# A third slot for split weights, and the two halves of a split issued in separate calls

## The chip, the cores and the metric

The kernel runs on one core of a Trainium2 chip. The metric is the device time in microseconds (us) of one execution; the figure for a kernel is the median of its runs. The engines of the core are named as in the profile: PE (matrix multiply), PEld (its weight loads, beside PE), DVE (vector), ACT (scalar), POOL (GpSimd) and SP (sync), from whose queue all DMAs here are issued.

## The reference

The reference computes, in fp32, two blocks over a sequence of 512 tokens with 1024 features, of which the first has two layers. It is cut here to what the matrix products are.

```
def first_block(x, mem, ...):                  # x: 512 x 1024, mem: 256 x 1024
    mem_n = rmsnorm(mem, mem_norm_g)
    for i in range(2):
        h = rmsnorm(x, norm_g[i])
        if i == 0: proj = h @ fox_w_in;  main = fox_attention(q, k, v, f_logit, b_f)
        else:      proj = h @ ret_w_in;  main = retention(q, k, v)
        memo = mem_cross_attention(q_mem, mem_n, w_mem_kv[i])
        x = x + (concat(main, memo) * silu(z)) @ w_out[i]
    return rmsnorm(x, final_norm_g)

def second_block(x, ...):
    h = rms_norm(x, norm_mix_pre)
    q, k, v, glu_in, gates = split(h @ w_in)
    y_a = dilated_attention(q, k, v, rel_bias) @ w_attn_out    # three groups, merged by their maxima and sums
    y_c = silu(layer_norm(causal_depthwise_conv(c_val * sigmoid(c_gate)))) @ conv_pw_w
    x = x + rms_norm((g_a * y_a + g_c * y_c) @ w_out, norm_mix_post)
    h = rms_norm(x, norm_ffn_pre)
    ...                                                         # gated FFN of width 2816, a conv of width 3
```

## The kernel before

Each fp32 product is made from three matmuls of split values: a value is its rounded high part h and the rest l, and a product sums h times h, h times l and l times h (mm3, L213 to L215; L422 to L424 for products laid out the other way round). Activations are split when they are written. Weights are split as they come: a job is one tile of weights of 1 MB. pump loads it (L314, on SP's queue) into one of two slots of ring_w; ACT copies it with rounding into the h half of a slot of ring_hl (L324, "the cast"), and DVE, for a few pieces POOL, subtracts that from the raw tile into the l half (L326, "the subtraction"). A job is split in two pieces as a rule. A slot of ring_hl holds h and l of a job, 2 x 2048 numbers of 4 bytes in each partition, 16 KiB; there are N_HL of them. When its last piece is split, the raw slot is free and pump loads the next job.

run_jobs goes through the list of jobs. A job with weights has one or more units, each a group of matmuls that fills a bank of psum and an evacuation of it. Before each unit and after the last one, cut_ahead(i, 1) splits one piece of a job to come, where a slot of ring_hl is free; after each unit, run_bg issues steps of background chains (norms, rotations, softmaxes, convolutions). This order of the text is not the final one: a scheduler puts the instructions on the queues of the engines, each of which then runs in order. Its result is what the rows of order in the section on the change show.

Places to which the text comes, by their lines:

- the first memory softmax, at 60 to 74 us: the exponentials L762 on ACT after a load of their table, the reciprocal L771 on DVE, the scaling L774 on POOL, and the transposes L782 on PE; L205 and L206 are a cast and a subtraction that split an activation, L876 a function of ACT in the chain of the forget gates;
- the entry to retention, at 528 to 570 us: L818 adds the last output projection of the first layer to x, L601 and L606 square and sum for the norm's statistic (L220 on PE, L230 on DVE, L231 on POOL), L519 and L694 split the memory's tiles, and the norm is applied to each of 8 tiles of x in L269 (product), L270 (its cast) and L271 (its subtraction, every second one on POOL); L678 adds projections;
- the exchanges of the three attention groups, four times from 1040 to 1345 us. They need maxima and sums of one group in the layout of another. Each writes them in L1541 and L1542 (to xn and xp in memory) and reads them back in L1547 and L1548, all on SP's queue; DVE makes coefficients from them (L1554 to L1563), POOL scales the probabilities with these (L1570), and PE transposes them (L1585). L1418 is the convolution on DVE, L1676 and L1682 store and fetch values of V in another order.

Of the kernel before, what the change touches and what calls it, by code (L numbers as in the profile page):

```python
# [11 lines left out]
F32 = mybir.dt.float32  # L12
# [22 lines left out]

N_R = 50
N_F = 23
N_HL = 2


class Slots:
# [59 lines left out]
def tile_kernel(ctx: ExitStack, tc: tile.TileContext, a: dict, out: bass.AP, stop_at=None):  # L101
    nc = tc.nc
# [8 lines left out]
    ring_w = cpool.tile([P, 2, 2048], F32, name="ring_w")  # L111
    ring_hl = cpool.tile([P, N_HL, 2, 2048], F32R, name="ring_hl")
    psum = ppool.tile([P, 8, 512], F32, name="psum")
# [3 lines left out]
    WS = Slots([ring_w[:, i] for i in range(2)], "W")  # L117
    WHL = Slots([ring_hl[:, i] for i in range(N_HL)], "WHL")
    PA = Slots([psum[:, i] for i in range(8)], "PA")
# [164 lines left out]
    chains = []  # L284
    once = deque()
    bg2 = deque()
    state = {"next": 0, "cut": 0, "rate": 1}

    def rate(n):
        state["rate"] = n  # L290
# [15 lines left out]
    def pump():  # L306

        while WS.q and state["next"] < len(weighted):
            j = weighted[state["next"]]
            state["next"] += 1  # L310
            j.w = WS.get()
            v = j.w.ap.rearrange("p (k c) -> p k c", k=j.shape[0])
            for sl, src in j.loads:
                nc.sync.dma_start(v[sl], src)  # L314

    def cut(j):

        if j.done == 0:
            j.s = WHL.get()
            j.hv = j.s.ap[:, 0].rearrange("p (k c) -> p k c", k=j.shape[0])  # L320
            j.lv = j.s.ap[:, 1].rearrange("p (k c) -> p k c", k=j.shape[0])
        v = j.w.ap.rearrange("p (k c) -> p k c", k=j.shape[0])
        sl = j.cut[j.done]
        nc.scalar.copy(j.hv[sl], v[sl])  # L324
        lo = j.hv[:, :, j.beside : 2 * j.beside] if j.beside else j.lv[sl]
        (nc.gpsimd if j.done in j.spare else nc.vector).tensor_sub(lo, v[sl], j.hv[sl].bitcast(F32))  # L326
        j.done += 1
        if j.done == len(j.cut):
            j.w.free()
            state["cut"] += 1  # L330
            pump()

    def cut_ahead(i, n):

        while n and state["cut"] < len(weighted) and state["cut"] <= i + 2:
            j = weighted[state["cut"]]
            if j.done == 0 and not WHL.q:
                return
            cut(j)
            n -= 1  # L340

    def run_bg():
        live = [c for c in chains if c.q]
        n = max(state["rate"], 1 if sum(len(c.q) for c in live) < 8 else 2)
        for c in live[:n]:
            c.q.popleft()()
        chains[:] = [c for c in chains if c.q]
        for _ in range(2):
            if once:
                once.popleft()()  # L350
        if bg2:
            bg2.popleft()()
# [7 lines left out]
    def run_jobs():  # L360
        i = -1
        for j in all_jobs:
            if j.loads is None:
                for u in j.units:
                    u()
                continue
            i += 1
            while state["cut"] <= i:
                cut(weighted[state["cut"]])
            if j.keep:  # L370
                continue
            for u in j.units:
                cut_ahead(i, 1)
                u(j.hv, j.lv)
                run_bg()
            for k in j.also + [j]:
                k.s.free()
            cut_ahead(i, 1)

    all_jobs = []  # L380
    weighted = []
# [1836 lines left out]
    weighted.extend(j for j in all_jobs if j.loads is not None)  # L2218
    prologue()
    run_jobs()  # L2220


# [53 lines left out]
```

## Time and profile before

| | |
|---|---|
| median of 3 runs | 1916.74 us (1914.56 to 1917.31) |
| the profiled execution | 1914.26 us, of which its span in the profile is 1912.5 us |
| PE busy | 1855.5 us, 97% of the span |
| DVE, ACT, POOL busy | 1134.0, 825.5 and 368.2 us |
| mean granted clock of PE | 0.990 |

Busy time is time in which an engine runs an instruction; the rest of its span it waits. The clock is given as a share of the full rate, 2.4 GHz. All places are given in us from the start of the span.

### The profile page before, as it was taken

What the parts mean: (1) busy time and instruction counts of PE and PEld (TensorE: products, weight loads), DVE (VectorE), ACT (ScalarE), POOL (GpSimd) and SP (SyncE); (2) the same over time, 40 slices, a digit from 0 to 9 for tenths busy, and PEclk for the clock granted to TensorE, in tenths of its full rate; (3) what the DMA queues carried; (4) which work ended last, traced back from release to release, by engine and by line L of the source; (5) the groups of instructions that cost most, each with busy time, mean ns of one, the idle gap of its engine ahead of it and who ended that gap; (6) DMA issues with size and microseconds to landing.
All of it is one profiled execution on the core that took longest, in us unless ns stands there. A gap on an engine that the chain in (4) does not pass through costs nothing. (4 is left out here: it accounts for less than half of the span.)

```text
span 1912.5 us, 24641 instructions
## 1 busy us (share of the span) xinstructions
PE 1855.5 (97%) x9759; PEld 1587.8 (83%) x9759; DVE 1134.0 (59%) x1752; ACT 825.5 (43%) x1389; POOL 368.2 (19%) x360
## 2 busy tenths in 40 slices
PE   7999999999989999999999998999899999999998
PEld 7788888888888888888878986988788887888886
DVE  7643543434474575755579797777365386554555
ACT  5544433444345545454353342335263455333342
POOL 1101000110131134333460202010131242100101
PEclk9999999999999999999999998999999999999999
DMA  6332322232233223323224432263553223323221
GB/s 207 115 119 87 100 77 89 79 99 91 86 114 101 94 78 100 100 77 99 67 72 145 137 100 72 59 179 68 167 170 113 89 67 101 109 88 111 88 90 65
DMA packets 200374, 194.57 MB, mean 102 GB/s; under 512 B 22200, under 2 KB 171575, under 8 KB 200259
## 3 DMA queue, kind: packets, MB, share of 16 engines
q1 hardware_dynamic: 200258, 193.00, 32.3%
q8 instruction: 76, 1.25, 0.3%
q14 instruction: 40, 0.32, 0.1%
HBM read 182.40 MB, written 12.94 MB: 102 GB/s over the span
## 5 line engine op out<-in xcount | busy, mean ns | idle before, releaser
L213 PE MATMUL psum<-arena_r,ring_hl 128*128 128x512 f32 (+1 forms) x1936 | 746.9, 387 | 1.8 <-ACT arena_r L1904 1.3
L215 PE MATMUL psum<-arena_r,ring_hl 128*128 128x512 f32 (+1 forms) x1936 | 740.1, 383 | 5.1 <-DVE ring_hl L326 5.1
L214 PE MATMUL psum<-arena_r,ring_hl 128*128 128x512 f32 (+1 forms) x1936 | 740.4, 383 | 3.4 <-DVE arena_r L627 2.6
L326 DVE TENSOR_TENSOR ring_hl<-ring_w,ring_hl 128x1024 fp32r<-128x1024 f32 (+2 forms) x306 | 394.6, 1296 | 303.0 <-ACT ring_hl L324 297.8
L324 ACT CAST ring_hl<-ring_w 128x1024 fp32r<-128x1024 f32 (+2 forms) x307 | 316.0, 1037 | 485.5 <-PE psum L214 315.4
L215 PEld LDWEIGHTS psum<-arena_r,ring_hl 128*128 128x128 f32 x1936 | 365.8, 189 | 77.3 <-DVE ring_hl L326 6.3
L214 PEld LDWEIGHTS psum<-arena_r,ring_hl 128*128 128x128 f32 x1936 | 366.4, 189 | 73.1 <-DVE arena_r L627 3.3
L213 PEld LDWEIGHTS psum<-arena_r,ring_hl 128*128 128x128 f32 x1936 | 366.3, 189 | 71.3 <-issue 1.9
L422 PE MATMUL psum<-ring_hl,arena_r 128*128 128x256 f32 x640 | 183.6, 287 | 2.2 <-ACT ring_hl L324 2.2
L424 PE MATMUL psum<-ring_hl,arena_r 128*128 128x256 f32 x640 | 182.9, 286 | 1.3 <-DVE ring_hl L326 1.3
L423 PE MATMUL psum<-ring_hl,arena_r 128*128 128x256 f32 x640 | 182.7, 285 | 0.0
L1418 DVE SCALAR_TENSOR_TENSOR arena_f<-cpad,vec,arena_f 128x512 f32<-128x512 f32 x240 | 173.8, 755 | 1.7
L422 PEld LDWEIGHTS psum<-ring_hl,arena_r 128*128 128x128 f32 x640 | 124.5, 194 | 3.4 <-ACT ring_hl L324 2.6
L424 PEld LDWEIGHTS psum<-ring_hl,arena_r 128*128 128x128 f32 x640 | 124.3, 194 | 1.8 <-DVE ring_hl L326 1.8
L423 PEld LDWEIGHTS psum<-ring_hl,arena_r 128*128 128x128 f32 x640 | 124.5, 194 | 0.5
L206 DVE TENSOR_TENSOR arena_r<-psum,arena_r 128x512 fp32r<-128x512 f32 (+2 forms) x136 | 79.3, 607 | 71.3 <-ACT arena_r L205 71.1
L205 ACT CAST arena_r<-psum 128x512 fp32r<-128x512 f32 (+2 forms) x136 | 66.9, 526 | 85.7 <-PE psum L215 35.2
L205 ACT CAST arena_r<-arena_f 128x512 fp32r<-128x512 f32 (+1 forms) x78 | 46.2, 598 | 117.0 <-POOL arena_f L1950 67.3
L926 POOL TENSOR_SCALAR arena_f<-arena_f,small 128x512 f32<-128x512 f32 (+3 forms) x48 | 34.1, 728 | 307.7 <-DVE small L924 302.4
L206 DVE TENSOR_TENSOR arena_r<-arena_f,arena_r 128x512 fp32r<-128x512 f32 (+1 forms) x78 | 53.3, 688 | 60.1 <-ACT arena_r L205 59.4
L606 POOL TENSOR_TENSOR arena_f<-arena_f 128x512 f32<-128x512 f32 x40 | 63.7, 1603 | 109.6 <-ACT arena_f L601 107.3
L1950 POOL TENSOR_TENSOR arena_f<-arena_f 128x512 f32<-128x512 f32 x22 | 32.0, 1456 | 262.2 <-DVE arena_f L1926 252.2
(238 smaller groups left out, 2093.3 us busy)
## 6 DMA issues: line engine op xcount, KB each, us to landing
ring_w<-in_fox_w_in SPq DMA_DIRECT2D x28, 1024.0 KB
ring_w<-in_w_in SPq DMA_DIRECT2D x22, 1024.0 KB
ring_w<-in_w_up SPq DMA_DIRECT2D x22, 1024.0 KB
ring_w<-in_w_out SPq DMA_DIRECT2D x20, 1024.0 KB
ring_w<-in_ret_w_in SPq DMA_DIRECT2D x16, 1024.0 KB
ring_w<-in_w_in SPq DMA_DIRECT2D x24, 512.0 KB
ring_w<-in_w_down SPq DMA_DIRECT2D x10, 1024.0 KB
ring_w<-in_w_mem_kv SPq DMA_DIRECT2D x8, 1024.0 KB
```

The lines of the kernel that those rows point to most:

```text
L205: nc.scalar.copy(h, src)
L206: nc.vector.tensor_sub(l, src, h.bitcast(F32))
L213: nc.tensor.matmul(ps, wh, xh, start=start and k == 0, stop=False, **o)
L214: nc.tensor.matmul(ps, wh, xl, start=False, stop=False, **o)
L215: nc.tensor.matmul(ps, wl, xh, start=False, stop=stop and k == n - 1, **o)
L324: nc.scalar.copy(j.hv[sl], v[sl])
L326: (nc.gpsimd if j.done in j.spare else nc.vector).tensor_sub(lo, v[sl], j.hv[sl].bitcast(F32))
L422: nc.tensor.matmul(o, c.h[:, sl], h[:, k, :], start=k == 0, stop=False)
L423: nc.tensor.matmul(o, c.l[:, sl], h[:, k, :], start=False, stop=False)
L424: nc.tensor.matmul(o, c.h[:, sl], l[:, k, :], start=False, stop=k == n - 1)
L606: nc.gpsimd.tensor_add(acc, acc, t.ap)
L1418: nc.vector.scalar_tensor_tensor(t, src, wk, t, ALU.mult, ALU.add)
```

## The change

There are three slots in ring_hl in place of two. The 16 KiB per partition for the third are taken from the scratch for dynamic DMAs, which is given 1024 bytes. The function cut is divided: cast() issues the cast of a piece and notes the piece in a list, halves; lower() takes the oldest from there and issues its subtraction. cut_ahead issues first the subtraction of the piece cast at the call before, and then the next cast. A job is cast if it lies at most two ahead of the running one, is loaded or being loaded, and has a slot. Every engine gets the same instructions as before. In the changed program lines above 313 keep their numbers; the cast is L326 (L324 before), the subtraction L338 (L326 before), and all later lines of the kernel have 14 more.

```diff
-N_HL = 2
+N_HL = 3
...
+    halves = deque()
+    state = {"next": 0, "cast": 0, "cut": 0, "rate": 1}
...
-    def cut(j):
-
+    def cast():
+
+        j = weighted[state["cast"]]
         if j.done == 0:
             j.s = WHL.get()
...
         sl = j.cut[j.done]
         nc.scalar.copy(j.hv[sl], v[sl])
-        lo = j.hv[:, :, j.beside : 2 * j.beside] if j.beside else j.lv[sl]
-        (nc.gpsimd if j.done in j.spare else nc.vector).tensor_sub(lo, v[sl], j.hv[sl].bitcast(F32))
+        halves.append((j, j.done))
         j.done += 1
         if j.done == len(j.cut):
+            state["cast"] += 1
+
+    def lower():
+
+        j, n = halves.popleft()
+        v = j.w.ap.rearrange("p (k c) -> p k c", k=j.shape[0])
+        sl = j.cut[n]
+        lo = j.hv[:, :, j.beside : 2 * j.beside] if j.beside else j.lv[sl]
+        (nc.gpsimd if n in j.spare else nc.vector).tensor_sub(lo, v[sl], j.hv[sl].bitcast(F32))
+        if n == len(j.cut) - 1:
             j.w.free()
             state["cut"] += 1
             pump()
 
     def cut_ahead(i, n):
 
-        while n and state["cut"] < len(weighted) and state["cut"] <= i + 2:
-            j = weighted[state["cut"]]
-            if j.done == 0 and not WHL.q:
-                return
-            cut(j)
+        while n:
             n -= 1
+            if halves:
+                lower()
+            c = state["cast"]
+            if c < len(weighted) and c <= i + 2 and c < state["next"] and (weighted[c].done or WHL.q):
+                cast()
...
             while state["cut"] <= i:
-                cut(weighted[state["cut"]])
+                if not halves:
+                    cast()
+                lower()
...
-    nc = bacc.Bacc("TRN2", target_bir_lowering=False, num_devices=1)
+    nc = bacc.Bacc("TRN2", target_bir_lowering=False, num_devices=1, dynamic_dma_scratch_size=1024)
```

On DVE, at the entry to retention, this stood from the norm's statistic L230 on (L326 is the subtraction of a piece of weights):

```order
L230 TENSOR_SCALAR small<-psum 128x4
L326 TENSOR_TENSOR ring_hl<-ring_w,ring_hl 128x8x128
L694 SCALAR_TENSOR_TENSOR arena_r<-psum,small,arena_r 128x256
L269 SCALAR_TENSOR_TENSOR arena_f<-arena_f,vec 128x512
L694 SCALAR_TENSOR_TENSOR arena_r<-psum,small,arena_r 128x256
L269 SCALAR_TENSOR_TENSOR arena_f<-arena_f,vec 128x512
L271 TENSOR_TENSOR arena_r<-arena_f,arena_r 128x512
L269 SCALAR_TENSOR_TENSOR arena_f<-arena_f,vec 128x512 x3
L694 SCALAR_TENSOR_TENSOR arena_r<-psum,small,arena_r 128x256
L271 TENSOR_TENSOR arena_r<-arena_f,arena_r 128x512
L326 TENSOR_TENSOR ring_hl<-ring_w,ring_hl 128x8x128
```

And in the changed program, from a little earlier on (L832 is L818 of before, L533 is L519, L708 is L694, and L338 the subtraction):

```order
L338 TENSOR_TENSOR ring_hl<-ring_w,ring_hl 128x8x128
L832 TENSOR_TENSOR arena_f<-psum,arena_f 128x512
L533 SCALAR_TENSOR_TENSOR arena_r<-psum,vec,arena_r 128x256 x5
L230 TENSOR_SCALAR small<-psum 128x4
L533 SCALAR_TENSOR_TENSOR arena_r<-psum,vec,arena_r 128x256
L338 TENSOR_TENSOR ring_hl<-ring_w,ring_hl 128x8x128
L708 SCALAR_TENSOR_TENSOR arena_r<-psum,small,arena_r 128x256
L269 SCALAR_TENSOR_TENSOR arena_f<-arena_f,vec 128x512
L708 SCALAR_TENSOR_TENSOR arena_r<-psum,small,arena_r 128x256
L269 SCALAR_TENSOR_TENSOR arena_f<-arena_f,vec 128x512
L271 TENSOR_TENSOR arena_r<-arena_f,arena_r 128x512
L269 SCALAR_TENSOR_TENSOR arena_f<-arena_f,vec 128x512 x2
```

The first subtraction after L230 of before stands ahead of the last L818 now, and the next one, which stood behind five L269 and two L271, has its place after L230.

On DVE, at the third exchange, the order was this (L1554 is the first instruction that reads what an exchange brought):

```order
L1418 SCALAR_TENSOR_TENSOR arena_f<-cpad,vec,arena_f 128x512 x3
L1554 TENSOR_TENSOR small<-small 128x4
L1418 SCALAR_TENSOR_TENSOR arena_f<-cpad,vec,arena_f 128x512
L1555 TENSOR_TENSOR small<-small 128x4
L1418 SCALAR_TENSOR_TENSOR arena_f<-cpad,vec,arena_f 128x512
L1557 TENSOR_TENSOR small<-small 128x12
L1418 SCALAR_TENSOR_TENSOR arena_f<-cpad,vec,arena_f 128x512
L326 TENSOR_TENSOR ring_hl<-ring_w,ring_hl 128x1024 x2
L1418 SCALAR_TENSOR_TENSOR arena_f<-cpad,vec,arena_f 128x512
L1554 TENSOR_TENSOR small<-small 128x4
```

In the changed program it is this (L1432 is L1418, L1568 is L1554):

```order
L1432 SCALAR_TENSOR_TENSOR arena_f<-cpad,vec,arena_f 128x512 x3
L1568 TENSOR_TENSOR small<-small 128x4
L1432 SCALAR_TENSOR_TENSOR arena_f<-cpad,vec,arena_f 128x512
L1569 TENSOR_TENSOR small<-small 128x4
L1432 SCALAR_TENSOR_TENSOR arena_f<-cpad,vec,arena_f 128x512
L1571 TENSOR_TENSOR small<-small 128x12
L1432 SCALAR_TENSOR_TENSOR arena_f<-cpad,vec,arena_f 128x512
L1568 TENSOR_TENSOR small<-small 128x4
L1573 TENSOR_TENSOR small<-small 128x12
```

The two subtractions between the first L1554 and the second have moved ahead of both.

On SP's queue, at the first exchange, the order was this:

```order
L1541 DMA xn<-small 128x4x1
L1457 DMA arena_f<-tdr 128x128
L1541 DMA xn<-small 128x4x1
L1547 DMA small<-xn 128x4 x2
L1676 DMA vdr<-arena_f 128x2x256
L314 DMA ring_w<-in_w_in 128x8x256
L1682 DMA arena_f<-vdr 128x512 x2
```

In the changed program it is this (L1555 is L1541, L1561 is L1547, L1690 and L1696 are L1676 and L1682, and L315 is the load of weights):

```order
L1555 DMA xn<-small 128x4x1
L1561 DMA small<-xn 128x4
L1555 DMA xn<-small 128x4x1
L315 DMA ring_w<-in_w_in 128x8x256
L1690 DMA vdr<-arena_f 128x2x256
L315 DMA ring_w<-in_w_in 128x8x128 x2
L1696 DMA arena_f<-vdr 128x512 x2
L1690 DMA vdr<-arena_f 128x2x256
L1561 DMA small<-xn 128x4
```

The second write stands behind the first read now, and the second read behind three loads of weights and three other kinds of transfer.

## Rows read from the trace of the kernel before

**Rows 1.** The page: head, busy time, DMA queues, costliest groups, DMA issues.

```profile
span 1912.5 us, 24641 instructions
...
PE 1855.5 (97%) x9759; PEld 1587.8 (83%) x9759; DVE 1134.0 (59%) x1752; ACT 825.5 (43%) x1389; POOL 368.2 (19%) x360
...
q1 hardware_dynamic: 200258, 193.00, 32.3%
...
L326 DVE TENSOR_TENSOR ring_hl<-ring_w,ring_hl 128x1024 fp32r<-128x1024 f32 (+2 forms) x306 | 394.6, 1296 | 303.0 <-ACT ring_hl L324 297.8
L324 ACT CAST ring_hl<-ring_w 128x1024 fp32r<-128x1024 f32 (+2 forms) x307 | 316.0, 1037 | 485.5 <-PE psum L214 315.4
...
ring_w<-in_fox_w_in SPq DMA_DIRECT2D x28, 1024.0 KB
```

**Rows 2.** Who waited for whom: total us, times, longest us.

```profile
ACT ring_hl L324 <- PE psum L214: 315.4, 116, 10.1
...
DVE ring_hl L326 <- ACT ring_hl L324: 297.8, 139, 10.7
```

**Rows 3.** The same, for PE alone.

```profile
PE psum L1585 <- POOL arena_f L1570: 15.5, 4, 7.0
...
PE psum L215 <- DVE ring_hl L326: 5.1, 4, 2.7
PE psum L782 <- POOL arena_f L774: 2.9, 2, 1.8
...
PE psum L424 <- DVE ring_hl L326: 1.3, 2, 1.1
```

**Rows 4.** Timeline of PE, 558 to 570: start, us, what, wait before it.

```profile
559.59 0.39 PE L215 MATMUL psum<-arena_r,ring_hl 128*128 128x256 f32 x1 [1.42 <-DVE ring_hl L326]
...
568.50 0.50 PE L215 MATMUL psum<-arena_r,ring_hl 128*128 128x512 f32 x1 [2.65 <-DVE ring_hl L326]
568.83 0.39 PE L213 MATMUL psum<-arena_r,ring_hl 128*128 128x512 f32 x1
...
569.53 0.39 PE L213 MATMUL psum<-arena_r,ring_hl 128*128 128x512 f32 x1
```

**Rows 5.** Timeline of DVE, 528 to 570.

```profile
534.05 1.54 DVE L326 TENSOR_TENSOR ring_hl<-ring_w,ring_hl 128x1024 fp32r<-128x1024 f32 x1 [1.64 <-ACT ring_hl L324]
...
547.78 1.23 DVE L326 TENSOR_TENSOR ring_hl<-ring_w,ring_hl 128x1024 fp32r<-128x1024 f32 x1 [7.16 <-ACT ring_hl L324]
...
558.33 1.21 DVE L326 TENSOR_TENSOR ring_hl<-ring_w,ring_hl 128x1024 fp32r<-128x1024 f32 x1
...
566.22 2.22 DVE L326 TENSOR_TENSOR ring_hl<-ring_w,ring_hl 128x1024 fp32r<-128x1024 f32 x1
```

**Rows 6.** Timeline of POOL, 60 to 570.

```profile
67.44 4.74 POOL L774 TENSOR_SCALAR arena_f<-arena_f,small 128x256 f32<-128x256 f32 x4 [4.05 <-DVE small L771]
...
566.09 1.27 POOL L271 TENSOR_TENSOR arena_r<-arena_f,arena_r 128x512 fp32r<-128x512 f32 x1 [1.28 <-ACT arena_r L270]
```

**Rows 7.** Timeline of DVE, 1224 to 1237.

```profile
1232.33 0.16 DVE L1554 TENSOR_TENSOR small<-small 128x4 f32<-128x4 f32 x1 [7.97 <-DMA small<-xp]
...
1234.65 2.35 DVE L326 TENSOR_TENSOR ring_hl<-ring_w,ring_hl 128x1024 fp32r<-128x1024 f32 x2
```

**Rows 8.** Timeline of ACT, 57 to 69.

```profile
62.35 1.05 ACT L324 CAST ring_hl<-ring_w 128x1024 fp32r<-128x1024 f32 x1 [1.26 <-PE psum L214]
```

**Rows 9.** Windows: busy us (instructions) by engine, granted clock, DMA share, GB/s.

```profile
540.38:543.79 3.41, 3.41 (x18) 3.41 (x17) 0.24 (x2) 0.00 (x0) 1.03 (x1) 0.50 0.90 305
```

**Rows 10.** Timeline of SP's DMA queue, 1045 to 1075.

```profile
1049.26 0.45 SPq L1541 DMA_DIRECT2D xn<-small  x1
...
1059.63 1.47 SPq L1547 DMA_DIRECT2D small<-xn  x2
```

**Rows 11.** Timeline of POOL, 1060 to 1080.

```profile
1066.01 11.35 POOL L1570 TENSOR_SCALAR arena_f<-arena_f,small 128x256 f32<-128x256 f32 x12 [20.04 <-ACT arena_f L1674]
```

**Rows 12.** Timeline of PE, 1100 to 1104.

```profile
1102.27 1.04 PE L1585 MATMUL psum<-ident,arena_f 128*128 128x128 f32 x8
```

More of the change, by code (lines that the diff above doesn't have):

```diff
@@ L286, in tile_kernel @@
     bg2 = deque()
-    state = {"next": 0, "cut": 0, "rate": 1}
+    halves = deque()
+    state = {"next": 0, "cast": 0, "cut": 0, "rate": 1}
     def rate(n):
```

## The prediction

> **What bounds the kernel now.** I read the page's head first, then who waits for whom, then the PE's own waits, and last the stretches around them. The reader is to see in [rows 1] that PE is busy 1855.5 of 1912.5 us, with DVE at 59% and ACT at 43%. So PE is the bound, and a change to how weights are split can only give what PE now loses: its gaps and its stretches at the lower clock. The largest waits of the two engines that split belong to the edited lines [rows 2]: ACT's cast L324 waits 315.4 us for PE's L214, because a job's slot in ring_hl comes free only when PE has read it, and DVE's subtraction L326 waits 297.8 us for that cast. They look like the prize, but they are waits of engines that idle anyway. What PE itself waits for is [rows 3]: 15.5 us for L1570 (the softmax's weights, which hang on transfers between groups), 5.1 us in L215 and 1.3 us in L424 for L326, 2.9 us in L782 for L774. Only the 6.4 us under L326 are late weights. That is 0.33% of the span, and it caps the direct gain.
>
> **The change, part by part.**
>
> *The scratch.* Nearly all packets are in q1, and all the rows of DMA issues, of which one stands in [rows 1], name SPq: nothing is issued from POOL or ACT. A smaller scratch for dynamic DMAs has no instruction that would use it, and I cost it at 0. The Trainium skill ("SBUF — State Buffer", SBUF size) says that this scratch is the ring of descriptors for DMAs that GpSimd issues; no run here shows what its size costs where it is used.
>
> *The third slot and the two calls.* Every engine keeps its instructions: 307 casts of 1037 ns and 306 subtractions of 1296 ns [rows 1]. What changes is when they stand in the queues. With two slots the splits are done one job ahead of PE; with three the rule allows two, about 11 us more (48 matmuls of 128x512 at 0.23 us, from the two starts in [rows 4], 0.70 us for three). In the steady projections a split is ready before PE needs it in both kernels, so the ACT and DVE waits that vanish there are worth 0; the cover is PE's own work on the job in between. The gain is where a split now arrives late, at these places.
>
> *Entry to retention.* PE loses 1.42 us before 559.59 and 2.65 us before 568.50 [rows 4]. DVE shows why: its subtraction at 547.78 stood 7.16 us for a cast that stood for a slot, and the next two stand behind the normalisation's L269, L271 and L694, so that they run at 558.33 and 566.22 [rows 5]. In the changed order one subtraction more stands ahead of L230, and the one that ran at 558.33 stands ahead of the first L269. The first stall, 1.42, goes. The second needs the subtraction of 566.22, whose predecessors are now one subtraction (1.2 us), one L271 (0.7) and one L678 (0.4) fewer, 2.3 us in all: it starts at about 563.9 and ends at 565.1. PE wants it at 568.50 - 2.65 - 1.42 = 564.4. That leaves 0.7 us if the normalisation starts no earlier than now; it starts earlier if ACT and DVE no longer stand behind the cast (7.16 us), and then nothing is left. I take the full 4.07, with 3.4 as the lower bound. Next after it could be h itself: POOL's last L271 ends at 567.36 [rows 6]; PE, entering the job at 563.8 and taking one of 8 tiles in 0.70 us, wants the last at 568.7. Not late.
>
> *Third group exchange.* PE loses 1.1 us in L424 (the longer of 1.3 us in two) [rows 3]: the two subtractions that it needs run at 1234.65 because they are queued behind L1554, which waits 7.97 us for a transfer [rows 7]. In the changed order they are gone from behind L1554; the next job's stand there, ready for a job that starts some 12 us later. Gain 1.1.
>
> *The rest of L215's 5.1 us* is 1.0 in two stalls, near 50 and 1547 us, where DVE's order keeps its subtractions. 0, at most 1.0.
>
> *First memory softmax (60 to 74).* PE loses 2.9 us for POOL's L774 [rows 3]. Ahead of it ACT waits 1.26 us in a cast at 62.35 for PE [rows 8]; that wait goes. But on ACT four casts now stand between L205 (the one before L876) and L762's table load where two stood, at 1.04 us each. So the softmax comes between 1.3 us earlier and 2.1 us later. I take 0, as the ends nearly cancel. The skill bears on this place, and it would change the time (rival 2).
>
> *The clock.* Before entry to retention the granted clock is 0.50 (the lower level, 1.2 GHz) from 540.38 to 543.79 [rows 9], 3.41 us, which costs PE 1.7 us. The work ahead of it, a subtraction at 534.05 that waits 1.64 us for its cast with L818 behind it [rows 5], comes sooner, but PE's small matmuls are moved forward too. 0, at most 1.7 gained.
>
> Sum: -4.07 - 1.1 = -5.2 us on the profiled 1914.26 us, 1909.1. That execution lies 2.5 us under the median of the three runs (1916.74), so the median should be 1911.6, 0.27% faster. About 0.2% (3.8 us) is what a measurement of this kernel can tell from no change.
>
> **Rivals.**
>
> *1. Hidden or given back: same.* A stall of 4 us at entry to retention is removed, but the softmax at 60 to 74 gives back 2.1, and 0.7 stays. Then -2.4 us, 1914.3. For it: ACT's four casts are certain, and a cast can now stand for a load instead of for PE. Against: L762's inputs are themselves ready only when PE has made them.
>
> *2. More than the sum.* L774 on POOL takes 4.74 us for four of 128x256 [rows 6], while three subtractions run on DVE; two stand together there afterwards and the third behind a copy that waits for PE. One subtraction less on DVE (1.2 us) would end L774 1.2 us sooner, and PE would lose 1.7 instead of 2.9. With the clock's 1.7 and the 1.0 left in L215 this gives -9.1 us, 1907.6. By the Trainium skill ("SBUF — State Buffer", the shared GPSIMD/Vector port) an operation of VectorE with two SBUF inputs and one of GpSimd that reads SBUF exclude each other for a whole instruction; the 4.74 us for four fit that, and by that rule the sum would be 6.4 and not 5.2.
>
> *3. Slower: the first group exchange.* SP is a queue in order. Before, both scatters L1541 are issued, then both reads L1547; the first read starts at 1059.63, 10.4 us after the first scatter at 1049.26 [rows 10]. In the changed order the second scatter stands behind the first read, so it starts at 1060, its data is there at about 1070, and its read stands behind weight loads, L1676 and L1682: some 1072. POOL's twelve L1570 end now at 1077.4 [rows 11]; the eight that need the later read (7.6 us of the 11.35) would end near 1090. PE wants them in L1585 at 1102.27 [rows 12], or 1097 after the gain ahead. That leaves 7 us. If the read, or DVE's coefficients behind it, come more than 7 us later than that, PE stalls as it does at the other exchanges: up to 7.0 us for the longest L1585 [rows 3], and then at 0.50 of the clock for at least 3.4 us, 1.7 lost. Against the sum: +8.7 - 5.2 = +3.5 us; with loads held up behind the same queue, and so a late weight of 2.65 as at 568.50, +6.2: 1922.9. For it: DVE has two waits in a row there with subtractions behind them. Against: 7 us of slack, and by count the subtractions ahead of the second wait are as many as before (166 and 166).
>
> *4. No effect.* The scheduler could have absorbed it; but at the two places its order has moved. The median would stay at 1916.7.
>
> **How the numbers follow.** The sum as above (-3.9 to -7 us): 0.45. Rival 1 (-3.8 to +1): 0.25. Rival 2 (below -7): 0.14. Rival 3 (over +3.8): 0.12. Rival 4: 0.04. Faster by over 0.2% takes in the sum and rival 2, 0.58 with rounding; slower is rival 3 with a little for unseen stalls, 0.13; same is 0.29. The predicted time is that of the sum, 1911.6. The range reaches down to rival 2 with the whole of L774's stall gone too (-9.1 and another 1.7: 1906) and up through rivals 1 and 4, to 1918; what lies outside is rival 3 and a few per cent below.
>
> **What would show it.** ACT's 315 us on L214 and DVE's 298 us on L324 fall by more than half, while PE's busy time stays within a few us: that the waits were cover. L215's and L424's waits for L326 fall from 6.4 us to 1 or 2. PE's gaps at entry to retention and at the third exchange are gone, and later work starts about 5 us sooner. L1585 still loses some 15 us. The prediction is wrong if a new wait for L1570, L774 or a late load stands among PE's, if another stretch at 0.50 appears, or if the 4.07 us are still there because the subtractions wait there for casts that wait for loads.

## The result, and the profile after

The changed kernel takes 1927.11 us (median of 5 runs, 1923.48 to 1931.72); the kernel before, on the same chip, 1916.74 us (5 runs, 1913.15 to 1917.69). The ratio is 1.0056, with a 95% interval of 1.0041 to 1.0071: 10.4 us slower by the medians, where 5 us faster were forecast. It lies outside the range given.

The page of the changed kernel, its head and busy times, and the two groups that split weights (L338 is the subtraction, L326 the cast):

```profile
span 1929.9 us, 24671 instructions
...
PE 1862.8 (97%) x9759; PEld 1596.0 (83%) x9759; DVE 1135.1 (59%) x1752; ACT 824.1 (43%) x1389; POOL 365.5 (19%) x360
...
L338 DVE TENSOR_TENSOR ring_hl<-ring_w,ring_hl 128x1024 fp32r<-128x1024 f32 (+2 forms) x306 | 394.2, 1294 | 295.9 <-ACT ring_hl L326 290.7
L326 ACT CAST ring_hl<-ring_w 128x1024 fp32r<-128x1024 f32 (+2 forms) x307 | 316.3, 1037 | 479.1 <-PE psum L214 298.6
```

Set against [rows 1], the head alone sorts the loss. The span is 17.4 us longer (this execution, of 1931.72 us, is the slowest of the five). PE's idle time, span less busy, goes from 57.0 to 67.1 us: 10.1 us. PE's busy time grows by 7.3 us with the same 9759 matmuls: that is the clock, whose mean falls from 0.990 to 0.983. So in this pair of executions about three fifths are new waits, and the rest is the lower clock behind them. A pair says this only roughly: e1_scratch below, with before's order on every engine, reads 60.7 us idle and 1861.0 busy, and e9_change_again, the changed kernel once more, 71.4 and 1864.0. In the mean of the two pairs PE is idle 10.4 us longer and busy 5.2 us longer, which makes two thirds new waits. The counts and the mean durations of casts and subtractions are those of before.

What PE waits for now, in total, times and longest:

```profile
PE psum L1599 <- POOL arena_f L1584: 22.8, 4, 10.9
PE psum L529 <- DMA arena_f<-in_mem: 6.2, 3, 4.6
PE psum L220 <- POOL arena_f L620: 4.3, 2, 2.3
PE psum L796 <- POOL arena_f L788: 3.8, 1, 3.8
PE psum L213 <- ACT arena_r L205: 3.5, 1, 3.5
...
PE psum L215 <- DVE ring_hl L338: 2.1, 2, 1.4
...
PE psum L438 <- DVE ring_hl L338: 0.3, 1, 0.3
```

The reader is to see that the wait the change was costed for did fall: L215's 5.1 us and L424's 1.3 us (L438 now) of [rows 3] are 2.1 and 0.3 us. What is shown above it grew or is new, but for L529's wait for an input, 6.2 us in both: the exchanges (L1599 is L1585) from 15.5 to 22.8 us, L220 and L213, which had no such entry of this size, and L796 (L782) from 2.9 to 3.8 us.

The two entry stalls of [rows 4] are gone, but at both sides of them stand others. POOL and PE just before the entry (L620 is L606, the sum of squares of the norm's statistic):

```profile
534.59 1.74 POOL L620 TENSOR_TENSOR arena_f<-arena_f 128x512 f32<-128x512 f32 x1 [1.83 <-ACT arena_f L615]
536.71 2.37 POOL L338 TENSOR_TENSOR ring_hl<-ring_w,ring_hl 128x1024 fp32r<-128x1024 f32 x1 [0.38 <-PE psum L529]
539.03 1.27 POOL L620 TENSOR_TENSOR arena_f<-arena_f 128x512 f32<-128x512 f32 x1
```

```profile
540.35 0.89 PE L220 MATMUL psum<-ones,arena_f 128*128 128x1 f32 x4 [2.35 <-POOL arena_f L620]
...
577.85 0.42 PE L213 MATMUL psum<-arena_r 128*128 128x256 f32 x1 [3.47 <-ACT arena_r L205]
```

A piece that POOL subtracts has moved ahead of the last L620. It takes POOL 2.37 us, and PE's L220 waits 2.35 us for the sum behind it. The wait of 3.47 us at 577.85 has its cause on ACT:

```profile
575.32 1.99 ACT L326 CAST ring_hl<-ring_w 128x1024 fp32r<-128x1024 f32 x2 [2.33 <-DMA ring_w<-in_ret_w_in]
577.22 0.58 ACT L205 CAST arena_r<-psum 128x512 fp32r<-128x512 f32 x1
```

Two casts stand ahead of L205 in ACT's queue and wait 2.33 us for a load. PE needs L205, and not yet the weights. The granted clock around these places and the exchanges (columns as in [rows 9]):

```profile
540.54:547.37 6.83, 6.83 (x33) 6.83 (x33) 0.55 (x2) 0.00 (x0) 1.03 (x1) 0.50 0.45 149
1175.36:1189.01 13.65, 5.77 (x17) 4.61 (x18) 13.40 (x26) 2.46 (x4) 11.07 (x13) 0.50 0.34 104
1349.50:1363.10 13.60, 6.10 (x18) 4.83 (x19) 5.98 (x14) 5.67 (x8) 7.79 (x13) 0.50 0.67 230
1564.50:1571.30 6.80, 6.80 (x34) 6.80 (x34) 1.39 (x2) 1.47 (x2) 1.02 (x1) 0.50 0.12 41
```

The stretch at 0.50 (1.2 GHz) behind the statistic is 6.83 us long, where it was 3.41 us [rows 9]; the one at 1564.5 us, at the start of the FFN, was not there. Each of the four begins in a gap of PE or just behind one.

The second exchange, before and after: SP's writes and reads of xn, and PE's first transposes. Before:

```profile
1143.69 0.36 SPq L1541 DMA_DIRECT2D xn<-small  x1
1153.79 0.91 SPq L1547 DMA_DIRECT2D small<-xn  x1
...
1171.26 1.11 PE L1585 MATMUL psum<-ident,arena_f 128*128 128x128 f32 x4 [6.16 <-POOL arena_f L1570]
```

After (L1555, L1561 and L1599):

```profile
1150.93 0.36 SPq L1555 DMA_DIRECT2D xn<-small  x1
1162.81 0.33 SPq L1561 DMA_DIRECT2D small<-xn  x1
...
1181.22 1.12 PE L1599 MATMUL psum<-ident,arena_f 128*128 128x128 f32 x4 [10.90 <-POOL arena_f L1584]
```

PE arrives at its transposes at 1171.26 - 6.16 = 1165.10 before, 21.41 us after the first write; with the change at 1170.32, 19.39 us after it. I call this time the lead. It has shrunk by 2.0 us, and the first read comes 11.88 us after the write in place of 10.10.

### The profile page after: what moved, and what is told of

Read it like the earlier page. It is cut to its first block, busy times and chain, and to the rows that moved or that the text cites. A ratio compares the mean times of both kernels' runs of the same rounds, so it can differ in the third digit from the quotient of the medians.

```text
span 1929.9 us, 24671 instructions
## 1 busy us (share of the span) xinstructions
PE 1862.8 (97%) x9759; PEld 1596.0 (83%) x9759; DVE 1135.1 (59%) x1752; ACT 824.1 (43%) x1389; POOL 365.5 (19%) x360
## 5 line engine op out<-in xcount | busy, mean ns | idle before, releaser
L213 PE MATMUL psum<-arena_r,ring_hl 128*128 128x512 f32 (+1 forms) x1936 | 749.0, 387 | 0.7 <-ACT arena_r L640 0.5
L215 PE MATMUL psum<-arena_r,ring_hl 128*128 128x512 f32 (+1 forms) x1936 | 742.6, 384 | 2.1 <-DVE ring_hl L338 2.1
L338 DVE TENSOR_TENSOR ring_hl<-ring_w,ring_hl 128x1024 fp32r<-128x1024 f32 (+2 forms) x306 | 394.2, 1294 | 295.9 <-ACT ring_hl L326 290.7
L326 ACT CAST ring_hl<-ring_w 128x1024 fp32r<-128x1024 f32 (+2 forms) x307 | 316.3, 1037 | 479.1 <-PE psum L214 298.6
L215 PEld LDWEIGHTS psum<-arena_r,ring_hl 128*128 128x128 f32 x1936 | 367.8, 190 | 73.5 <-DVE ring_hl L338 2.8
L213 PEld LDWEIGHTS psum<-arena_r,ring_hl 128*128 128x128 f32 x1936 | 368.4, 190 | 70.8 <-issue 1.9
L438 PE MATMUL psum<-ring_hl,arena_r 128*128 128x256 f32 x640 | 183.2, 286 | 0.3 <-DVE ring_hl L338 0.3
L437 PE MATMUL psum<-ring_hl,arena_r 128*128 128x256 f32 x640 | 183.1, 286 | 0.0
L1432 DVE SCALAR_TENSOR_TENSOR arena_f<-cpad,vec,arena_f 128x512 f32<-128x512 f32 x240 | 174.4, 760 | 1.4
L437 PEld LDWEIGHTS psum<-ring_hl,arena_r 128*128 128x128 f32 x640 | 124.9, 195 | 0.5
L438 PEld LDWEIGHTS psum<-ring_hl,arena_r 128*128 128x128 f32 x640 | 124.7, 195 | 0.6 <-DVE ring_hl L338 0.6
L206 DVE TENSOR_TENSOR arena_r<-psum,arena_r 128x512 fp32r<-128x512 f32 (+2 forms) x136 | 79.3, 607 | 63.5 <-ACT arena_r L205 63.4
L205 ACT CAST arena_r<-psum 128x512 fp32r<-128x512 f32 (+2 forms) x136 | 66.9, 526 | 86.5 <-PE psum L215 33.0
L205 ACT CAST arena_r<-arena_f 128x512 fp32r<-128x512 f32 (+1 forms) x78 | 46.2, 597 | 126.9 <-POOL arena_f L1964 72.2
L206 DVE TENSOR_TENSOR arena_r<-arena_f,arena_r 128x512 fp32r<-128x512 f32 (+1 forms) x78 | 53.5, 691 | 64.0 <-ACT arena_r L205 64.0
L620 POOL TENSOR_TENSOR arena_f<-arena_f 128x512 f32<-128x512 f32 x40 | 64.1, 1613 | 108.5 <-ACT arena_f L615 102.3
```

Of the source, the lines that this page charges most:

```text
L205: nc.scalar.copy(h, src)
L206: nc.vector.tensor_sub(l, src, h.bitcast(F32))
L213: nc.tensor.matmul(ps, wh, xh, start=start and k == 0, stop=False, **o)
L215: nc.tensor.matmul(ps, wl, xh, start=False, stop=stop and k == n - 1, **o)
L338: (nc.gpsimd if n in j.spare else nc.vector).tensor_sub(lo, v[sl], j.hv[sl].bitcast(F32))
L437: nc.tensor.matmul(o, c.l[:, sl], h[:, k, :], start=False, stop=False)
```

## The experiments

The kernels that follow change lines ahead of the places that are spoken of, so line numbers shift by up to 4 in most of them (L1589 and L1574 there are L1585 and L1570 of before); those made from the changed kernel keep its numbers. All ratios are to the kernel before on the same chip, with 95% intervals.

**The parts of the change alone.** Four kernels. The first is before with the small scratch only, the second has the third slot too and the old cut in one call, the third is the changed kernel with two slots, the fourth the changed kernel with a tighter limit.

```diff
# e1_scratch, from before
-    nc = bacc.Bacc("TRN2", target_bir_lowering=False, num_devices=1)
+    nc = bacc.Bacc("TRN2", target_bir_lowering=False, num_devices=1, dynamic_dma_scratch_size=1024)
# e2_slot, from e1_scratch
-N_HL = 2
+N_HL = 3
# e3_apart, from the changed kernel
-N_HL = 3
+N_HL = 2
# e4_one_ahead, from the changed kernel
-            if c < len(weighted) and c <= i + 2 and c < state["next"] and (weighted[c].done or WHL.q):
+            if c < len(weighted) and c <= i + 1 and c < state["next"] and (weighted[c].done or WHL.q):
```

> The kernel before with the smaller scratch alone; every engine's order is that of before. Depth theory (the loss comes from splits that stand one job deeper in the queues of DVE, ACT and POOL, ahead of chains that PE waits for) and calls theory (the loss comes from issuing cast and subtraction apart): both expect no change, ratio 0.999 to 1.001 to before. Scratch theory (the size of the scratch itself costs time): about 1927 us, ratio 1.005 or more.

Measured: 1.0005 [0.9994, 1.0016]. The scratch costs nothing that can be measured here. The profile of this kernel, whose instructions and order are those of before, also shows how far single executions differ; its page and its waits have

```profile
PE 1861.0 (97%) x9759; PEld 1592.0 (83%) x9759; DVE 1133.6 (59%) x1752; ACT 825.1 (43%) x1389; POOL 368.8 (19%) x360
```

```profile
PE psum L1585 <- POOL arena_f L1570: 20.4, 4, 9.8
```

where [rows 1] and [rows 3] have 1855.5 and 15.5 us. The profiled execution of before has the lowest figure of both among all kernels here.

> The kernel before with the third slot and the smaller scratch, but cast and subtraction in one call as before. Depth theory: most of the loss is there, ratio 1.004 to 1.008, with PE's waits for L1570 above 20 us (15.5 before). Calls theory: no loss, ratio 0.997 to 1.001.

Measured: 1.0075 [1.0056, 1.0093]. The slot alone, with cast and subtraction still in one call, is slower, and by the waits of the changed kernel:

```profile
PE psum L1585 <- POOL arena_f L1570: 25.3, 4, 12.4
...
PE psum L220 <- POOL arena_f L606: 4.3, 2, 2.4
...
PE psum L213 <- ACT arena_r L205: 2.5, 1, 2.5
```

> The changed kernel with two slots: cast and subtraction apart, depth as before. Depth theory: near before, ratio 0.998 to 1.002, and L1585's waits for POOL near 15 us. Calls theory: the loss of the changed kernel, ratio 1.004 to 1.007.

Measured: 1.0046 [1.0029, 1.0063]. The split into two calls alone is slower as well, in another place: PE waits 14.8 us in L215 for L338, and 6.54 us of that stand at the first exchange. SP and DVE there:

```profile
1059.63 0.33 SPq L1561 DMA_DIRECT2D small<-xn  x1
...
1074.00 0.42 SPq L1561 DMA_DIRECT2D small<-xn  x1
```

```profile
1071.72 0.16 DVE L1568 TENSOR_TENSOR small<-small 128x4 f32<-128x4 f32 x1 [15.51 <-DMA small<-xn]
...
1080.77 1.22 DVE L338 TENSOR_TENSOR ring_hl<-ring_w,ring_hl 128x1024 fp32r<-128x1024 f32 x1
```

```profile
1082.04 0.80 PE L215 MATMUL psum<-arena_r,ring_hl 128*128 128x512 f32 x1 [6.54 <-DVE ring_hl L338]
```

The second read starts 14.4 us after the first, behind other transfers, as rival 3 had it. But what PE waits for is not the exchange. DVE stands 15.51 us for the first read, and the subtraction that PE wants stands behind that in its queue, the "late weight" that rival 3 priced at 2.65 us. With three slots the second read is as late (17.3 us after the first in the changed kernel), and PE has no such wait, since the subtractions of that job have already run.

> The changed kernel with three slots, but a cast may stand only one job ahead (c at most i + 1), so that the cast never waits for PE to free a slot and the subtractions stand no deeper than before. Depth theory: near before or faster, ratio 0.996 to 1.001; ACT's waits for PE's L214 fall below 100 us. Calls theory: ratio 1.004 to 1.007. Slot theory (more SBUF for splits is what costs): ratio above 1.004.

Measured: 1.0069 [1.0052, 1.0086]; the exchanges cost PE 25.5 us. The expectation failed: the tighter limit left the scheduled depth as it was. By the trace DVE has as many subtractions ahead of the last statistics of exchanges 2, 3 and 4 as with the change (182, 192 and 208; before 180, 190 and 206). Here the slots decide how far ahead the scheduler puts a split, not the limit in the text. That a third slot costs merely by being there is excluded by e6_first_block below, which has one too.

**The third slot only where it is wanted.** These start from before, with three slots and a function that says which jobs may take the last free slot. Other jobs leave one free, so that their order stays that of before.

```diff
+    def third(k):
+        return k in (44, 95)      # e5_select; e6_first_block: k < 71; e7_second_block: k >= 71
...
-            j.s = WHL.get()
+            j.s = WHL.get(0 if third(state["cut"]) else min(1, len(WHL.q) - 1))
...
-            if j.done == 0 and not WHL.q:
+            if j.done == 0 and len(WHL.q) < (1 if third(state["cut"]) else 2):
```

> The kernel before with three slots, of which the third is used for two jobs alone: the last one of the memory's keys and values before retention, and the one that PE waits for at the third exchange. All other jobs alternate between two slots as before; PE's order is that of before. Place theory (the third slot lets the scheduler move every split two subtractions forward, which pays at two places and costs at others: entry to retention, the FFN, POOL's queue): the two gains without the costs, 4 to 5 us less, ratio 0.9965 to 0.9985; L215's waits for DVE's subtraction about 1 us, L424's below 0.4. Contention theory (a split anywhere earlier costs DVE and ACT time that shows later): ratio 0.999 to 1.003.

Measured: 1.0011 [1.0002, 1.0020], a miss for the place theory and inside the range of the contention theory, which isn't tested further. Job 44 is the one whose subtraction was late at the entry, job 95 that at the third exchange. The 1.42 us stall goes and the third exchange's 1.1 us too (one of 0.9 us comes some 15 us later), but the next stall at the entry grows from 2.65 to 3.62 us. The cast that could now be early waits for its load:

```profile
545.96 1.05 ACT L328 CAST ring_hl<-ring_w 128x1024 fp32r<-128x1024 f32 x1 [7.62 <-DMA ring_w<-in_w_mem_kv]
```

ring_w still has two slots, so the load can't be issued sooner. For the cast of before that starts at nearly the same time, the one behind the 7.16 us of [rows 5], the profile names no releaser:

```profile
546.70 1.05 ACT L324 CAST ring_hl<-ring_w 128x1024 fp32r<-128x1024 f32 x1 [8.46 <-issue]
```

So what the prediction read as a wait for a slot was probably this load. With the whole change the loads there are issued earlier (the first of in_ret_w_in at 539 us in place of 552).

> The kernel before with the third slot used in the first block alone (its 71 jobs). Place theory: the gain of 4 us at entry to retention is eaten there by POOL's subtraction ahead of the last product for the norm (1.7 us, and one more stretch of 3.4 us at half clock) and by a cast that stands for a load (2 to 3.5 us and another stretch): ratio 1.001 to 1.004, and from the second block on no new gap. Second-block theory (the whole loss arises at the exchanges and in the FFN): ratio 0.997 to 1.000.

> The kernel before with the third slot used from the second block on alone. Place theory: the FFN's entry and its first convolution cost 2 to 3 us and one or two stretches at half clock, the third exchange gives 1: ratio 1.002 to 1.005. Second-block theory: ratio 1.005 to 1.009.

Measured: first block 0.9996 [0.9985, 1.0006], second block 1.0025 [1.0013, 1.0036]. What loss there is stands in the second block. The two halves make 1.0021 together, though, and e8_no_spare below, the changed kernel but for one piece, 1.0040 on the same chip, so they may not hold all of it. In the first, two small stalls near 900 us (1.8 us) and the entry's go, and L220's 2.35 us and an L213 of 2.47 us come, as in the changed kernel.

The changed kernel, with POOL's pieces given to DVE:

```diff
# e8_no_spare, from the changed kernel
-            all_jobs[n0 + 2].spare = (1,)
+            all_jobs[n0 + 2].spare = ()
```

> The changed kernel, with the one subtraction that POOL does (a piece of the memory's weights of the second layer) given to DVE. Place theory: L220 at entry to retention waits below 1 us for POOL's product instead of 2.35, and the stretch at half clock there is 3.4 us instead of 6.8; ratio 1.002 to 1.006. If POOL's place doesn't matter: ratio as the changed kernel's, 1.004 to 1.008, with the 2.35 us kept.

Measured: 1.0040 [1.0026, 1.0054]. L220 at the entry waits 1.07 us in place of 2.35:

```profile
537.17 1.05 PE L220 MATMUL psum<-ones,arena_f 128*128 128x1 f32 x8 [1.07 <-POOL arena_f L620]
```

POOL's moved piece is shown as the cause of that wait. The stretch at 0.50 behind it is 3.4 us in place of 6.8, but this isn't shown to come from the wait: e2_slot, e6_first_block and e9_change_again wait 2.35 to 2.4 us there and have a stretch of 3.4 us.

**The second block in parts.** On another chip, with the changed kernel again beside them:

```diff
-        return k in (44, 95)
+        return 71 <= k < 113      # e10_mix: to the end of the three groups
...
+        return k >= 113           # e11_ffn
...
+        return k < 71             # e12_first_dve, with POOL's pieces on DVE as in e8_no_spare
```

> The changed kernel as it is, beside its parts on one chip. If the parts add up: its ratio is that of the parts together (first block, mixing jobs, FFN), within 0.002. If there is a loss of its own in issuing cast and subtraction apart: 0.002 or more above the parts.

> The kernel before with the third slot used for the second block's mixing jobs alone (projections, exchanges, output). PE's order is that of before. Exchange theory (two subtractions more ahead of each exchange on DVE, which is full there, make L1541's data and L1570 late): L1585 waits 2 to 5 us longer in sum, the third exchange gains 1: ratio 1.001 to 1.004. FFN theory (the loss of the second block is the FFN's): ratio 0.998 to 1.000.

> The kernel before with the third slot used in the FFN alone. Exchange theory: ratio 0.999 to 1.001. FFN theory: PE's small matmuls for the norm's statistic (L220), which stand 13 matmuls earlier in PE's order, wait 1.9 us for POOL, a stretch of 6.8 us at half clock follows, and the first convolution's product waits 1.1 us for DVE: ratio 1.002 to 1.005.

> The third slot used in the first block alone, and POOL's one subtraction given to DVE. Place theory: the first block's gain of 4 us at entry to retention without most of the 2.35 us at L220: ratio 0.9975 to 0.9995, the fastest version so far. If POOL's place doesn't matter: as the first block alone with POOL, 0.999 to 1.001.

Measured: the change 1.0092 [1.0076, 1.0109], the mixing part 1.0052 [1.0038, 1.0065], the FFN part 1.0024 [1.0011, 1.0037], the first block 1.0001 [0.9992, 1.0011]. The parts add up to 1.0077, within the intervals of the whole. The size isn't the same everywhere, by more than the intervals allow: the whole is 1.0056 in the first measurement, and the jobs of the mixing part and the FFN together, 1.0076 here, were 1.0025 on the chip of e7_second_block. Why is not shown; ratios of one chip are compared below. The first block misses the 0.9975 to 0.9995 that were expected of it: L220's wait is down to 1.07 us, but L213's behind the two casts is 3.46, where e6_first_block has 2.35 and 2.47. The casts wait only 0.59 us for their load there, so their own 2 us ahead of L205 count as well. In the FFN part, PE's queue shows three new stalls, L215 behind DVE, L221 (L220) behind POOL's sum of squares, and L2040, of the first convolution, behind DVE:

```profile
1557.50 0.39 PE L215 MATMUL psum<-arena_r,ring_hl 128*128 128x256 f32 x1 [2.02 <-DVE arena_r L1909]
1560.03 1.23 PE L221 MATMUL psum<-ones,arena_f 128*128 128x1 f32 x5 [1.90 <-POOL arena_f L610]
...
1624.04 0.47 PE L2040 MATMUL psum<-ring_hl,arena_r 128*128 128x512 f32 x1 [1.15 <-DVE arena_f L1930]
```

The scheduler put L221 13 matmuls earlier in PE's queue there, 97 matmuls behind the group of L237 (L236) where before has 110, and the sum was not ready earlier. That it did so because the weights of other matmuls were now ready sooner is argued, not shown.

**The exchanges.** The suspected cause in the mixing part was that two more subtractions stand ahead of the last statistics of exchanges 2 and 4, on a DVE that is full (busy 34.75 of the 35.00 us from 1115 to 1150 before). One kernel gives the third slot to these two jobs alone, one to all others of the part; a third tries for a faster version.

```diff
+        return k in (90, 103)     # e13_two_jobs
...
+        return 71 <= k < 113 and not 88 <= k < 91 and not 101 <= k < 104      # e14_mix_but_exchanges
...
+        return k < 71 and k != 47 # e15_first_but_one, with POOL's pieces on DVE
```

> Third slot only for the weight jobs numbered 90 and 103, whose two subtractions then stand on DVE ahead of the last statistics of the second and the fourth exchange; all other instructions stand as before. If two subtractions on a full DVE make the exchanges late (what is argued of the mixing part), the time from the first xn write to PE's arrival at L1589 shrinks from about 21.4 and 21.1 us to 19.5 to 20.5 at exchanges 2 and 4, PE's wait for L1588's transposes' source grows from about 16 to 20 us or more, and the kernel is 1.003 to 1.005 of before. If the loss comes from the depth over the whole part (slot traffic, ACT, POOL, the clock), these four figures stay as before and the ratio is within 0.0015 of 1.

> The third slot over the whole mixing part (jobs 71 to 112) but for jobs 88 to 90 and 101 to 103, so that the subtractions ahead of the last statistics number 181 at the second exchange (180 before, 182 with the change) and 206 at the fourth (206 before, 208 with the change). If the place of those subtractions is the cause, the fourth exchange reads as before (lead about 21.1 us, wait about 8 us) and the second lies half way (lead about 20.5 to 21), with a ratio of 1.001 to 1.003, against 1.0052 for the whole part; if depth in the part as such is the cause, the ratio stays at 1.004 to 1.006.

Measured: 1.0013 [1.0002, 1.0025] for the two jobs alone, 1.0052 [1.0038, 1.0066] for everything but them. The second is the ratio that the whole part had on the other chip. So the theory in this narrow form falls: on one chip the two jobs cost a quarter of what everything but them costs. Exchange 2 in the two kernels, first the two jobs alone:

```profile
1149.22 1.11 SPq L1545 DMA_DIRECT2D xn<-small  x1
...
1178.68 1.12 PE L1589 MATMUL psum<-ident,arena_f 128*128 128x128 f32 x4 [9.12 <-POOL arena_f L1574]
```

```profile
1148.84 0.36 SPq L1545 DMA_DIRECT2D xn<-small  x1
...
1184.61 1.11 PE L1589 MATMUL psum<-ident,arena_f 128*128 128x128 f32 x4 [14.90 <-POOL arena_f L1574]
```

The lead is 20.34 us in the first and 20.87 us in the second, against 21.41 before: each does part of it. The fourth exchange of e14 has before's number of subtractions ahead of its last statistics, 206, and its lead is 20.29 us all the same. The wait of 14.90 us in e14 is the longest of all; PE starts 24.8 us behind the first read there, where the other kernels have 16.3 to 19.5. The same reading (start of the first xn write, start of PE's transposes less their wait) over all kernels, each in its one profiled execution, gives means in us:

| | lead, exchange 2 / 4 | write to PE's start | PE's wait |
|---|---|---|---|
| 7 with before's order there (before, e1, e5, e6, e11, e12, e15) | 21.4 / 21.3 | 29.2 / 29.0 | 7.8 / 7.7 |
| 8 with three slots there (after, e2, e4, e7 to e10, e14) | 20.1 / 20.0 | 31.0 / 30.1 | 10.9 / 10.1 |

The lead hardly varies in the first row of kernels (21.07 to 21.43). With three slots it is 19.4 to 21.3. So the statistics are written 1.3 us later against PE in the mean, and the way from the write to PE's start is 1.1 to 1.8 us longer besides, 5.5 us for the two exchanges, and the lower clock behind. All but 0.1 us of the longer way lies between the write and the read of it (10.6 to 12.5 us at exchange 2, 10.5 to 11.5 at exchange 4). What lengthens that is not settled. One execution can't say more: with before's order PE's waits for L1570 took from 15.5 to 20.4 us in all (17.8 in the mean), and with three slots from 18.9 to 26.7 (23.5). In e7, e10, e13 and e14 another 2.4 us stand in a wait near 47 us (below), ahead of any job that these kernels change, so their profiles, and perhaps their ratios, hold a loss that isn't the exchanges'.

> The third slot in the first block (jobs below 71) but for job 47, whose casts stood on ACT ahead of L205's copy at 570 us and waited there for their load; POOL's piece on DVE. If that cast is what gave the gain back, the stall of 2.5 to 3.5 us near 570 goes, the stalls of 1.42 and 2.65 us of before stay gone, and the kernel is 0.998 to 0.999 of before (a version ahead of both). If another late load takes its place, a stall of 2 us or more stands between 560 and 580 and the ratio is within 0.001 of 1.

Measured: 0.9989 [0.9979, 0.9998], the fastest kernel of the study, by about 2 us, though its interval ends close to 1. Job 47's casts are those ahead of L205. But the entry doesn't show the gain that was expected: the stall near 573 shrinks to 1.15 us, and a new one stands at the next softmax (L778 and L786 are L774 and L782).

```profile
573.03 0.39 PE L214 MATMUL psum<-arena_r 128*128 128x256 f32 x1 [1.15 <-ACT arena_r L206]
...
586.79 0.77 PE L786 MATMUL psum<-ident,arena_f 128*128 128x128 f32 x5 [2.14 <-POOL arena_f L778]
```

```profile
575.72 2.00 ACT L328 CAST ring_hl<-ring_w 128x1024 fp32r<-128x1024 f32 x2 [2.74 <-DMA ring_w<-in_ret_w_in]
```

The casts still wait for a load, 2.74 us, and then delay the softmax in place of L205. What it gains in its profile are the 1.8 us near 900 us; e6_first_block and e12_first_dve gain these too and measure no change, so what makes this kernel faster is open.

## Why the prediction was wrong

**What held.** The entry's 1.42 and 2.65 us and the third exchange's 1.1 us went, as the sum said; the waits of L215 and L424 for late weights fell by 4.0 of 6.4 us (one new one of 1.4 us stands near 42 us). They went although one reason given for the full 4.07 did not hold: DVE's wait of 7.16 us for a cast is still there, 8.44 us behind a cast that waits 10.35 us for PE's L437 (L423 before). The lower bound of 3.4 also took 1.2 us for a subtraction that [rows 5] has at 2.22; with that it is 2.4. The scratch is worth 0, shown by e1. Rival 3's second read did come late, and the slack of PE took it, as the argument against that rival had it.

**The step that failed** is "The gain is where a split now arrives late, at these places.", with the sentence ahead of it that puts every other moved split at 0 since "the cover is PE's own work on the job in between." It counts what a moved split gains. What stands behind it now is asked at the first softmax, where the term is 0, and in rival 3, and has no term in the sum anywhere else. Splits moved forward in queues that run in order, ahead of work that PE needs sooner than the weights. By place, in the profiled executions:

- *The second and fourth exchange*, said to stay at "some 15 us": 22.8 us, +7.3 in this pair and +5.7 in the means of the kernels in the table. The stretches at 0.50 there grew from 10.2 and 6.8 to 13.6 us each, but e1_scratch, with before's order, has 13.7 and 10.2. e10 places 1.0052 in the part that holds them. That DVE's statistics come later against PE is shown by the leads; that two subtractions do it alone is disproved by e13 and e14; the rest of the longer way is open. A gain forecast at 1.1 us for the third exchange was read from the same queue, two subtractions ahead of L1554, without asking for the statistics behind them.
- *The first block*: +1.7 us in L220, since POOL's piece was not followed (shown by e8); +3.5 us in L213 behind two casts of 2 us that also wait for a load. The prediction named "casts that wait for loads" as a sign of being wrong, but for late subtractions and not for a copy that stands behind those casts, and gave them no term. At the first softmax PE waits 0.9 us longer. L774 starts 2.1 us later, at the end of the bounds given, and takes 3.97 us in place of 4.74 with two subtractions beside it, the direction of rival 2. So the 4.1 us gained are given back: e6 and e12 measure no change.
- *The FFN*, where the prediction has no loss: 1.0024 by e11, with three new waits of 2.0, 1.9 and 1.2 us. One is for a statistic that PE's queue now reaches earlier than its sum is ready.
- *The clock*, "0, at most 1.7 gained": PE's busy time grew by 7.3 us in this pair and by 5.2 in the mean of the two pairs above. In all executions on the chip of e9_change_again the granted clock is 0.987 before and 0.982 with the change. The new gaps of 2.35, 3.47 and 1.92 us each have a stretch at half rate behind them; those of 1.35 us near 42 and of 1.47 us near 1630 have none.

**The sub-step on covered waits** failed too. ACT's wait for a slot and DVE's for the cast were to fall by more than half. They are 298.6 and 290.7 us, from 315.4 and 297.8 [rows 2]. The reason is argued from the program: a third slot lets a split run one job earlier once; after that a slot comes free only when PE has finished a job, as before, and ACT waits for that as long. e4 adds that the limit of jobs ahead in the text, on which the depth of "two, about 11 us more" was built, isn't what binds.

The chances had the right rival, slower, at 0.13, and for a mechanism that cost PE nothing in the changed kernel.

## What to carry to other kernels

Deeper lookahead for one operand isn't free because the engines that prepare it have time to spare on average: in queues that run in order, look at what each moved instruction is now ahead of, on every engine that takes part, and at what PE needs from there first. Look above all where an engine is full, as DVE is for 35 us ahead of the second exchange, and where the moved instruction can itself wait for a transfer. If PE is 97% busy, price a new gap at its length plus half of the half-rate stretch that follows it, where one does, and give the extra slot only to the part of the program where it measures as no loss.

## What was not expected of the hardware

The same POOL instruction in the same place of the order took 1.36 us before and 3.93 us in e13_two_jobs. In e13_two_jobs, POOL and DVE near 47 us (L272 is L271, L330 the subtraction, L207 is L206):

```profile
47.48 3.93 POOL L272 TENSOR_TENSOR arena_r<-arena_f,arena_r 128x512 fp32r<-128x512 f32 x1 [0.42 <-DMA arena_f<-in_conv_dw_b]
```

```profile
47.00 0.68 DVE L272 TENSOR_TENSOR arena_r<-arena_f,arena_r 128x512 fp32r<-128x512 f32 x1
47.60 1.22 DVE L330 TENSOR_TENSOR ring_hl<-ring_w,ring_hl 128x1024 fp32r<-128x1024 f32 x1
48.73 0.42 DVE L207 TENSOR_TENSOR arena_r<-arena_f,arena_r 128x256 fp32r<-128x256 f32 x1
49.07 1.22 DVE L330 TENSOR_TENSOR ring_hl<-ring_w,ring_hl 128x1024 fp32r<-128x1024 f32 x1
```

Before, it was the other way round:

```profile
47.89 1.36 POOL L271 TENSOR_TENSOR arena_r<-arena_f,arena_r 128x512 fp32r<-128x512 f32 x1 [0.43 <-ACT arena_r L270]
```

```profile
47.41 0.68 DVE L271 TENSOR_TENSOR arena_r<-arena_f,arena_r 128x512 fp32r<-128x512 f32 x1
48.01 2.32 DVE L326 TENSOR_TENSOR ring_hl<-ring_w,ring_hl 128x1024 fp32r<-128x1024 f32 x1
```

One of the two is stretched, POOL's to 3.93 us or DVE's from 1.22 to 2.32 us, and which one is not explained by their order of arrival: in both kernels POOL starts 0.48 us behind DVE's own L271 and 0.12 us ahead of the subtraction. PE waits 2.77 us where it is POOL's. The Trainium skill ("SBUF — State Buffer", section "SBUF: two separate sides") says that an operation of DVE with two inputs in SBUF, the memory of these tiles, and one of POOL that reads SBUF use one pair of ports, which the one that starts first holds for its whole instruction while the other blocks. The rows agree in that one of the two pays; they don't show which of them got the pair first.

A write of the small statistics and its read lay 9.8 to 14.1 us apart at exchange 2 in these executions, with the same bytes (the read waits for the write, and stands in one queue with other transfers): a spread of 4.4 us, where the whole change was expected to bring 5.
